# More visits to the wide chunks in the first stage of a transformer block kernel, and the key work moved behind it

## The chip, the cores and the metric

The kernel runs on one core of a Trainium2 chip. The metric is the device time of one execution in microseconds (us). The engines are called as the profile calls them: PE (TensorE, matrix products), DVE (VectorE), ACT (ScalarE), POOL (GpSimd) and SP (SyncE, whose queue issues nearly all DMAs here).

## What is computed

One layer of a diffusion backbone: 256 latent tokens `x` and 256 context tokens `ctx` of width 2048, all in fp32. The part that matters here, cut from the reference:

```python
shift, scale, gate = split(silu(c) @ w_mod + b_mod, 3)       # w_mod: 2048 x 6144
u   = layer_norm(x)   * (1 + scale)   + shift
u_c = layer_norm(ctx) * (1 + scale_c) + shift_c              # same w_mod, c_ctx
p   = u @ w_in                                               # all columns
p_c = u_c @ w_in[:, :N_KV]                                   # the key/value columns only
# columns: mLSTM q,k | mLSTM v | mLSTM gates | GQA k | GQA v | then o, z, q_b, z_b, g
q, k   = silu(conv3(qk_pre));  v = v_a                       # mLSTM inputs
k_b    = rope(rms_norm(k_b, k_norm_w))                       # GQA keys
h_a    = mlstm(q, k, v, gates);  o_attn = softmax(q_b k_b^T) v_b
out    = branch_merge(...) @ w_out;  x_new = layer_norm(ALPHA * x + gate * out)
```

The columns that both `x` and `ctx` need (mLSTM k, v and gates, GQA k and v) are the first stage of the kernel, up to about 419 us. The mLSTM q product, the heads, the attention, the merge and the output follow.

## The kernel before

A row tile is 128 of the 2048 rows that a product sums over; there are 16 of them (`KT`). An fp32 product is made of three products of rounded parts: weights and u are each split in a high half (`hi`, `whi`) and a low half (`lo`, `wlo`), and `three` (L336 to L338) or `three_b` (L341 to L343) multiplies high by high, high by low and low by high. A weight block holds two row tiles by 512 columns (128x1024, "wide"; 352 columns and 128x704 for w_kv, "narrow"), or one row tile where a visit begins or ends at an odd one. SP loads it (L312, tile `raw`, three buffers), ACT makes `whi` (L332), DVE makes `wlo` (L333); two blocks (`LEAD`) are split ahead of the one that PE multiplies.

The first stage has nine chunks of columns, in the list `chunks`: kv0, kv1, ka0, ka1, va0, va1, va2, va3, kv2. A product takes all 512 tokens, so a row tile of a chunk is 12 products (24 half as wide for ka). Each chunk sums in four PSUM banks (`four` takes the two sets of four in turn). Since u is made row tile by row tile, a chunk is visited twice: the first visits take row tiles 0 to `ENDS` (1, 1, 1, 3, 5, 6, 8, 9 and 10 of them), in which u is made; the second visits take the rest, in the same order of chunks. The first visit's sums are copied to SBUF by ACT, the second's are added there by DVE (`put`, L436 and L438). So the tenth visit, kv0's second, asks for row tiles 1 to 15 of u: all of them.

A row tile of u needs two columns of the modulation (shift and scale). For the first six (`MOD_PE`) PE makes them; for the ten others DVE does: four w_mod loads of 512 KB (`mod`, SP, L181), eight units (`mod_unit`, L221, tile `junk`), finishes (L227, L229), the normalised x (L254; for row tiles 12 to 15 it is loaded again as `xt`, L274), PE's transposes (`xT`, L286), and the split of u (ACT L298, DVE L299). These tasks are put in a list in program order: `end` is an estimate of PE's time by row tiles, and six tasks are given out for each `DT` us of it (11.5). `weave` spreads a visit's tasks over its products, four ticks a row tile. A scheduler then sets the order on each engine.

The 16 gate columns of the modulation are made in the same way, with two loads and two units each (`gate_task`), two columns in each second visit but the first (`GATES`). From the eleventh visit (`LATE`) on their loads take buffers from a later pool of three (`late`), in place of five. Three more pieces of work are woven into the second visits: `gates()` (mLSTM gate arithmetic, 13 steps), `conv_k` (one for each of eight heads, L637 to L641) and `keys()` (norm, rope and transposes of the GQA keys, ten steps, L657 to L705). The mLSTM q products (`w_qa`, two chunks of 16 row tiles, latent tokens only) come next with nothing woven in.

Of the kernel before, what the change touches and what calls it, by code (L numbers as in the profile page):

```python
# [17 lines left out]
KT = D // P  # L18
# [9 lines left out]
ALPHA = 2.0 ** 0.25  # L28
NEG = -1.0e30
BIG = 2064  # L30
ENDS = (1, 1, 1, 3, 5, 6, 8, 9, 10)
LATE = 1
GATES = (0, 2, 2, 2, 2, 2, 2, 2, 2)
MOD_PE = 6
AHEAD = 5
DEPTH = 3
# [1 line left out]
GAP = 1  # L38
LEAD = 2
SLOTS = (1, 2, 2, 4, 5)  # L40
T0, DT = 8.0, 11.5
SMALL = {1: 8, 2: 4, 4: 6, 16: 3}

C_ID, C_ONE, C_SEL, C_CAP, C_TRI = 0, P, 2 * P, 2 * P + 8, 5 * P + 8
# [4 lines left out]
def block_kernel(ctx: ExitStack, tc: tile.TileContext, a: dict, out: bass.AP):  # L49
# [33 lines left out]
    def acc(n):  # L83
        return ps.tile([P, 512], F32, tag="acc", name=nm(n))
# [4 lines left out]
    flip = [1]  # L89
# [216 lines left out]
    plan, early, ready = [], [], []  # L306
# [92 lines left out]
    def gemm_feat(w, kts, regions):  # L399


        for ks, _, _ in row_blocks(w, 512, kts):
            wh, wl = load_w()
            for b, k in enumerate(ks):
                for f in range(4):
                    tick()
                    need(k)
                    c0 = b * 512 + f * P
                    for s, o, first, last in regions[f]:
                        us = u[s][k // 4][:, k % 4]  # L410
                        three_b(o, wh[:, c0:c0 + P], wl[:, c0:c0 + P], turns(us[:, 0, :]),
                                turns(us[:, 1, :]), first and k == kts[0], last and k == kts[-1])
# [49 lines left out]
    def chunk_kv(c, kts, first):  # L462
# [5 lines left out]
        for t in range(4):  # L468
# [6 lines left out]
            else:  # L475
                put(vb[0][:, t, 160:512], tl[t][:, 0:352], first)

    chunks = [(chunk_kv, "w_kv", 0), (chunk_kv, "w_kv", 1), (chunk_ka, "w_ka", 0),
              (chunk_ka, "w_ka", 1), (chunk_va, "w_va", 0), (chunk_va, "w_va", 1),
              (chunk_va, "w_va", 2), (chunk_va, "w_va", 3), (chunk_kv, "w_kv", 2)]  # L480


    def row_tiles(g, c):
        return range(ENDS[c], KT) if g else range(ENDS[c])

    def prep_tasks(kt):

        ts = col_tasks(kt) if kt < MOD_PE else unit_tasks((kt, 16 + kt), (0, 1))
# [3 lines left out]
    def gate_task(j):  # L492
        return unit_tasks((j,), (0,)) + [lambda: mod_finish(j, (0,))]

    ln_stats()
    norm_x(0, 1)
    for g in range(2):
        for c, (_, w, i) in enumerate(chunks):
            plan.extend(b[1:] for b in row_blocks(a[w][i], 352 if w == "w_kv" else 512, row_tiles(g, c)))
    for ws in ([("w_qa", c)] for c in range(2)), ([("w_o", c), ("w_z", c)] for c in range(4)), \  # L500
            ([("w_qb", c), ("w_zb", c)] for c in range(4)), \
            ([("w_g", c), ("w_ba", c), ("w_g", 4 + c), ("w_bb", c)] for c in range(4)), \
# [1 line left out]
        for w, c in (x for l in ws for x in l):  # L504
            plan.extend(b[1:] for b in row_blocks(a[w][c], 512, range(KT)))
    tasks = queue(prep_tasks(0))
    between = [[] for _ in range(18)]
    for kt in range(1, MOD_PE):
        between[SLOTS[kt - 1]] += prep_tasks(kt)
    units = [t for kt in range(MOD_PE, KT) for t in prep_tasks(kt)]  # L510
    end, j = 0.0, 0
    for i in range(18):
        end += len(row_tiles(i // 9, i % 9)) * (1.8 if chunks[i % 9][1] == "w_kv" else 2.65)
        j0, j = j, max(j, min(len(units), math.ceil((end - T0) * 6 / DT)))
        between[i] = queue(mix(between[i], units[j0:j]))
    assert j == len(units)
# [398 lines left out]
    n = HEAD_STEPS  # L915
# [295 lines left out]
```

## Time and profile before

| | us |
|---|---|
| median of three runs | 1357.17 |
| lowest and highest | 1352.03, 1358.71 |
| profiled execution | 1356.43 |
| its span | 1354.7 |
| PE busy in the span | 1303.6 (96%) |
| DVE busy | 949.0 (70%) |
| ACT busy | 650.4 (48%) |

The profile is of one execution. The span runs from the first to the last instruction of the trace, and the 1.7 us between span and time lie around it. PE's busy time is a sum over listed instructions; matmuls overlap in the pipeline, so a busy PE isn't PE at its peak, and the granted clock (PEclk, 1.00 is the full one) has to be read beside it.

### The profile page before, as it was taken

What the parts mean: (1) busy time and instruction counts of PE and PEld (TensorE: products, weight loads), DVE (VectorE), ACT (ScalarE), POOL (GpSimd) and SP (SyncE); (2) the same over time, 40 slices, a digit from 0 to 9 for tenths busy, and PEclk for the clock granted to TensorE, in tenths of its full rate; (3) what the DMA queues carried; (4) which work ended last, traced back from release to release, by engine and by line L of the source; (5) the groups of instructions that cost most, each with busy time, mean ns of one, the idle gap of its engine ahead of it and who ended that gap; (6) DMA issues with size and microseconds to landing.
All of it is one profiled execution on the core that took longest, in us unless ns stands there. A gap on an engine that the chain in (4) does not pass through costs nothing. (4 is left out here: it accounts for less than half of the span.)

```text
span 1354.7 us, 19750 instructions
## 1 busy us (share of the span) xinstructions
PE 1303.6 (96%) x7613; PEld 1160.6 (86%) x7613; DVE 949.0 (70%) x1537; ACT 650.4 (48%) x929; POOL 44.9 (3%) x74
## 2 busy tenths in 40 slices
PE   5899999999999999999999999999999999999996
PEld 3678889999889988888889999898888888888885
DVE  6589997488745767788778778787555455544657
ACT  3544332154223667766665565666444444444441
POOL 0000000000100000100010000000000000000000
PEclk9999999999999999999999999999999999999998
DMA  8997768535435654445545354434756666576663
GB/s 301 331 326 246 234 210 290 201 124 196 161 110 162 190 193 157 164 167 169 190 148 186 128 169 143 153 125 160 215 200 202 201 195 208 191 281 219 213 219 121
DMA packets 77693, 264.16 MB, mean 195 GB/s; under 512 B 8904, under 2 KB 11608, under 8 KB 76960
## 3 DMA queue, kind: packets, MB, share of 16 engines
q1 hardware_dynamic: 75696, 256.19, 56.3%
q0 software_dynamic: 1296, 6.49, 1.4%
q8 instruction: 59, 0.97, 0.3%
q10 hardware_dynamic: 608, 0.24, 0.1%
q14 instruction: 34, 0.28, 0.1%
HBM read 260.75 MB, written 2.14 MB: 194 GB/s over the span
## 5 line engine op out<-in xcount | busy, mean ns | idle before, releaser
L333 DVE TENSOR_TENSOR wlo<-raw,whi 128x1024 fp32r<-128x1024 f32 (+2 forms) x374 | 444.7, 1192 | 296.0 <-ACT whi L332 295.7
L332 ACT CAST whi<-raw 128x1024 fp32r<-128x1024 f32 (+2 forms) x374 | 379.9, 1019 | 473.9 <-PE p L338 114.9
L336 PE MATMUL p<-whi,u 128*128 128x512 f32 (+1 forms) x448 | 158.7, 361 | 3.7 <-ACT u L298 2.8
L337 PE MATMUL p<-wlo,u 128*128 128x512 f32 (+1 forms) x448 | 159.5, 357 | 2.3 <-DVE wlo L333 2.1
L338 PE MATMUL p<-whi,u 128*128 128x512 f32 (+1 forms) x448 | 157.6, 355 | 0.0
L221 DVE SCALAR_TENSOR_TENSOR junk<-mod,sc 128x1024 bf16<-128x1024 f32 x112 | 134.2, 1219 | 10.0 <-DMA mod<-in_w_mod 9.7
L336 PEld LDWEIGHTS p<-whi,u 128*128 128x128 f32 x448 | 85.2, 192 | 15.5 <-ACT u L298 3.5
L337 PEld LDWEIGHTS p<-wlo,u 128*128 128x128 f32 x448 | 86.0, 192 | 11.2 <-DVE wlo L333 4.1
L338 PEld LDWEIGHTS p<-whi,u 128*128 128x128 f32 x448 | 85.9, 192 | 7.0 <-issue 0.4
L343 PE MATMUL p<-u,wlo 128*128 128x256 f32 x256 | 71.2, 278 | 2.3 <-DVE wlo L333 2.3
L341 PE MATMUL zb<-u,whi 128*128 128x256 f32 x256 | 72.1, 281 | 0.0
L341 PE MATMUL p<-u,whi 128*128 128x256 f32 x256 | 71.1, 278 | 0.0
L342 PE MATMUL p<-u,whi 128*128 128x256 f32 x256 | 70.8, 277 | 0.0
L343 PE MATMUL zb<-u,wlo 128*128 128x256 f32 x256 | 70.4, 275 | 0.0
L342 PE MATMUL zb<-u,whi 128*128 128x256 f32 x256 | 70.4, 275 | 0.0
L337 PE MATMUL z<-wlo,u 128*128 128x512 f32 x128 | 49.2, 384 | 4.3 <-DVE wlo L333 4.3
L337 PE MATMUL o<-wlo,u 128*128 128x512 f32 x128 | 49.1, 383 | 3.5 <-DVE wlo L333 3.4
L343 PEld LDWEIGHTS p<-u,wlo 128*128 128x128 f32 x256 | 49.5, 194 | 3.3 <-DVE wlo L333 2.5
L341 PEld LDWEIGHTS p<-u,whi 128*128 128x128 f32 x256 | 49.4, 193 | 0.4 <-issue 0.4
L336 PE MATMUL q<-whi,u 128*128 128x512 f32 x128 | 49.7, 388 | 0.0
L342 PEld LDWEIGHTS p<-u,whi 128*128 128x128 f32 x256 | 49.5, 193 | 0.0
L336 PE MATMUL ga<-whi,u 128*128 128x512 f32 x128 | 49.4, 386 | 0.0
(330 smaller groups left out, 3145.4 us busy)
## 6 DMA issues: line engine op xcount, KB each, us to landing
mod<-in_w_mod SPq DMA_DIRECT2D x96, 512.0 KB, 5.0
raw<-in_w_g SPq DMA_DIRECT2D x64, 512.0 KB, 4.3
raw<-in_w_o SPq DMA_DIRECT2D x32, 512.0 KB, 4.1
raw<-in_w_z SPq DMA_DIRECT2D x32, 512.0 KB, 4.2
raw<-in_w_qb SPq DMA_DIRECT2D x32, 512.0 KB, 3.9
raw<-in_w_zb SPq DMA_DIRECT2D x32, 512.0 KB, 3.5
raw<-in_w_ba SPq DMA_DIRECT2D x32, 512.0 KB, 3.5
raw<-in_w_bb SPq DMA_DIRECT2D x32, 512.0 KB, 4.1
```

Source lines behind the costliest of these rows:

```text
L221: nc.vector.scalar_tensor_tensor(junk, blk, 1.0, sc[v][:, hf * 1024:(hf + 1) * 1024], op0=ALU.mult, op1=ALU.mult, accum_out=mp[:, v, hf, j ...
L332: nc.scalar.copy(hi, src)
L333: nc.vector.tensor_tensor(lo, src, hi.bitcast(F32), op=ALU.subtract)
L336: mm(o, lhsT=xh, rhs=wh, start=start, stop=False)
L337: mm(o, lhsT=xh, rhs=wl, start=False, stop=False)
L338: mm(o, lhsT=xl, rhs=wh, start=False, stop=stop)
L341: mm(o, lhsT=wh, rhs=xh, start=start, stop=False)
L342: mm(o, lhsT=wh, rhs=xl, start=False, stop=False)
L343: mm(o, lhsT=wl, rhs=xh, start=False, stop=stop)
```

## The change

A table of 21 visits, (chunk, first row tile, end), takes the place of `ENDS`. The first nine are those of before. Then three wide chunks are visited again: va0 for row tiles 5 to 11, va1 for 6 to 12, va2 for 8 to 13. Only then comes kv0 for 1 to 15, then kv1, ka0 and ka1 as before, then third visits of va0 (12 to 15), va1 (13 to 15) and va2 (14 and 15), and va3 and kv2 as before. `DT` is 16 in place of 11.5. The later pool opens at the same place (kv1's second visit, now number 13). The gate columns are given out 3, 4, 3, 1, 1, 0, 2, 2 over the visits from kv1's on. The gate arithmetic is spread over kv1 to va0, `conv_k` of four heads goes to va3, of two to kv2, and the last two with all ten steps of `keys()` to the two q chunks, where the transposes now take PSUM banks of the other set (`flip[0] = 1`).

```diff
-ENDS = (1, 1, 1, 3, 5, 6, 8, 9, 10)
-LATE = 1
-GATES = (0, 2, 2, 2, 2, 2, 2, 2, 2)
+VISITS = ((0, 0, 1), (1, 0, 1), (2, 0, 1), (3, 0, 3), (4, 0, 5), (5, 0, 6), (6, 0, 8), (7, 0, 9),
+          (8, 0, 10), (4, 5, 12), (5, 6, 13), (6, 8, 14), (0, 1, 16), (1, 1, 16), (2, 1, 16),
+          (3, 3, 16), (4, 12, 16), (5, 13, 16), (6, 14, 16), (7, 9, 16), (8, 10, 16))
+LATE = 13
+GATES = (0,) * 13 + (3, 4, 3, 1, 1, 0, 2, 2)
...
-T0, DT = 8.0, 11.5
+T0, DT = 8.0, 16.0
...
-    for i in range(18):
-        end += len(row_tiles(i // 9, i % 9)) * (1.8 if chunks[i % 9][1] == "w_kv" else 2.65)
+    for i, (c, k0, k1) in enumerate(VISITS):
+        end += (k1 - k0) * (1.8 if chunks[c][1] == "w_kv" else 2.65)
...
-    for c, ts in enumerate(([], gs[:3], gs[3:6], [], gs[6:12], gs[12:] + cks[:4], cks[4:], ks[:3], ks[3:])):
-        between[9 + c] = mix(between[9 + c], ts)
+    for i, ts in enumerate((gs[:3], gs[3:6], gs[6:9], gs[9:11], gs[11:], [], cks[:4], cks[4:6])):
+        between[LATE + i] = mix(between[LATE + i], ts)
...
-        weave(between[i], 4 * len(kts))
-        fn(n, kts, i < 9)
+        weave(between[i], 4 * (k1 - k0))
+        fn(n, range(k0, k1), k0 == 0)
...
+    flip[0] = 1
+    for c, ts in enumerate((cks[6:] + ks[:4], ks[4:])):
         tl = [acc("qa") for _ in range(2)]
+        weave(ts, 32)
         gemm_feat(a["w_qa"][c], range(KT), regions_lat(tl))
+        flush()
```

The scheduler's order shows what moves. Up to about 64 us and from the second q chunk's middle on, the orders of the two kernels are the same on every engine. Names in the rows: `junk` is a unit, `mod` its loaded columns, `mv` a finish, `wlo` a split, `raw` a loaded block, `xt` an x tile; the numbers behind a name tell tiles apart and differ between the kernels.

**First place**, DVE, the normalisation of row tile 12's x. Before, it stands at the border of the first visits of va3 (the 128x512 block is its last) and kv2:

```order
L221 SCALAR_TENSOR_TENSOR junk_244_1291,mp_84<-mod_227_1187,sc_8_108 128x1024
L221 SCALAR_TENSOR_TENSOR junk_246_1305,mp_84<-mod_229_1201,sc_8_108 128x1024
L333 TENSOR_TENSOR wlo_248_1319<-raw_233_1226,whi_249_1320 128x512
L221 SCALAR_TENSOR_TENSOR junk_251_1325,mp_84<-mod_231_1215,sc_7_107 128x1024
L227 TENSOR_TENSOR mv_85<-mp_84 128x2
L221 SCALAR_TENSOR_TENSOR junk_251_1325,mp_84<-mod_231_1215,sc_8_108 128x1024
L221 SCALAR_TENSOR_TENSOR junk_254_1354,mp_84<-mod_236_1244,sc_7_107 128x1024
L333 TENSOR_TENSOR wlo_256_1365<-raw_240_1277,whi_257_1366 128x704
L254 TENSOR_SCALAR xt_252_1337<-xt_252_1337,ag0_148,rs0_147 128x128 x4
L221 SCALAR_TENSOR_TENSOR junk_254_1354,mp_84<-mod_236_1244,sc_8_108 128x1024
```

After, with kv2's first visit done, at the beginning of va0's second:

```order
L225 SCALAR_TENSOR_TENSOR junk_269_1497,mp_84<-mod_239_1307,sc_8_108 128x1024
L337 TENSOR_TENSOR wlo_266_1485<-raw_255_1402,whi_267_1486 128x512
L225 SCALAR_TENSOR_TENSOR junk_278_1534,mp_84<-mod_248_1338,sc_8_108 128x1024
L225 SCALAR_TENSOR_TENSOR junk_283_1557,mp_84<-mod_250_1364,sc_7_107 128x1024
L231 TENSOR_TENSOR mv_85<-mp_84 128x2
L225 SCALAR_TENSOR_TENSOR junk_283_1557,mp_84<-mod_250_1364,sc_8_108 128x1024
L337 TENSOR_TENSOR wlo_275_1528<-raw_260_1437,whi_276_1529 128x1024
L225 SCALAR_TENSOR_TENSOR junk_289_1598,mp_84<-mod_258_1420,sc_7_107 128x1024
L337 TENSOR_TENSOR wlo_280_1551<-raw_265_1483,whi_281_1552 128x1024
L258 TENSOR_SCALAR xt_284_1572<-xt_284_1572,ag0_148,rs0_147 128x128 x4
L225 SCALAR_TENSOR_TENSOR junk_289_1598,mp_84<-mod_258_1420,sc_8_108 128x1024
```

The normalisation now has two wide splits and a half one ahead of it among the units, where it had a half one and a narrow one.

**Second place**, DVE, the border of kv1 and ka0. The 128x512 block is ka0's first, the 128x704 block ahead of it kv1's last. Before:

```order
L221 SCALAR_TENSOR_TENSOR junk_426_2692,mp_84<-mod_424_2688,sc_7_107 128x1024
L333 TENSOR_TENSOR wlo_371_2134<-raw_361_2066,whi_372_2135 128x704
L221 SCALAR_TENSOR_TENSOR junk_431_2756,mp_84<-mod_425_2690,sc_7_107 128x1024
L227 TENSOR_TENSOR mv_85<-mp_84 128x1
L229 TENSOR_TENSOR mv_85<-mv_85,bm_74 128x1
L221 SCALAR_TENSOR_TENSOR junk_439_2876,mp_84<-mod_430_2754,sc_7_107 128x1024
L333 TENSOR_TENSOR wlo_374_2167<-raw_366_2100,whi_375_2168 128x512
L221 SCALAR_TENSOR_TENSOR junk_443_2938,mp_84<-mod_438_2874,sc_7_107 128x1024
L333 TENSOR_TENSOR wlo_381_2211<-raw_370_2132,whi_382_2212 128x1024
```

After:

```order
L225 SCALAR_TENSOR_TENSOR junk_446_2695,mp_84<-mod_438_2591,sc_7_107 128x1024
L337 TENSOR_TENSOR wlo_419_2472<-raw_408_2400,whi_420_2473 128x704
L225 SCALAR_TENSOR_TENSOR junk_451_2729,mp_84<-mod_445_2693,sc_7_107 128x1024
L231 TENSOR_TENSOR mv_85<-mp_84 128x1
L233 TENSOR_TENSOR mv_85<-mv_85,bm_74 128x1
L337 TENSOR_TENSOR wlo_423_2507<-raw_413_2436,whi_424_2508 128x512
L225 SCALAR_TENSOR_TENSOR junk_457_2818,mp_84<-mod_450_2727,sc_7_107 128x1024
L225 SCALAR_TENSOR_TENSOR junk_462_2852,mp_84<-mod_456_2816,sc_7_107 128x1024
L337 TENSOR_TENSOR wlo_430_2551<-raw_418_2470,whi_431_2552 128x1024
```

Two units and not one stand between the 128x512 split and the one behind it.

**Third place**, DVE, inside ka0's second visit. Before:

```order
L333 TENSOR_TENSOR wlo_392_2319<-raw_380_2209,whi_393_2320 128x1024
L227 TENSOR_TENSOR mv_85<-mp_84 128x1
L221 SCALAR_TENSOR_TENSOR junk_472_3196,mp_84<-mod_463_3123,sc_7_107 128x1024
L229 TENSOR_TENSOR mv_85<-mv_85,bm_74 128x1
L221 SCALAR_TENSOR_TENSOR junk_476_3229,mp_84<-mod_471_3194,sc_7_107 128x1024
L583 TENSOR_REDUCE m0_2575<-gc_389_2269 8x2
L227 TENSOR_TENSOR mv_85<-mp_84 128x1
L584 TENSOR_SCALAR m0_2575<-m0_2575 8x2
L229 TENSOR_TENSOR mv_85<-mv_85,bm_74 128x1
L221 SCALAR_TENSOR_TENSOR junk_489_3295,mp_84<-mod_487_3291,sc_7_107 128x1024
L221 SCALAR_TENSOR_TENSOR junk_495_3344,mp_84<-mod_488_3293,sc_7_107 128x1024
L333 TENSOR_TENSOR wlo_397_2377<-raw_386_2245,whi_398_2378 128x1024
```

After:

```order
L337 TENSOR_TENSOR wlo_448_2723<-raw_435_2585,whi_449_2724 128x1024
L231 TENSOR_TENSOR mv_85<-mp_84 128x1
L225 SCALAR_TENSOR_TENSOR junk_503_3314,mp_84<-mod_497_3246,sc_7_107 128x1024
L233 TENSOR_TENSOR mv_85<-mv_85,bm_74 128x1
L225 SCALAR_TENSOR_TENSOR junk_510_3386,mp_84<-mod_502_3312,sc_7_107 128x1024
L231 TENSOR_TENSOR mv_85<-mp_84 128x1
L225 SCALAR_TENSOR_TENSOR junk_520_3456,mp_84<-mod_518_3452,sc_7_107 128x1024
L233 TENSOR_TENSOR mv_85<-mv_85,bm_74 128x1
L337 TENSOR_TENSOR wlo_453_2783<-raw_442_2661,whi_454_2784 128x1024
L225 SCALAR_TENSOR_TENSOR junk_521_3483,mp_84<-mod_519_3454,sc_7_107 128x1024
```

Before, four units stand ahead of wlo_397 and none between it and the next splits; after, three stand ahead of wlo_453, as four do ahead of wlo_448 and three ahead of wlo_459.

## Rows read from the trace of the kernel before

**Rows 1.** The page, part 1: engine, busy us (share of the span), instructions.
```profile
PE 1303.6 (96%) x7613; PEld 1160.6 (86%) x7613; DVE 949.0 (70%) x1537; ACT 650.4 (48%) x929; POOL 44.9 (3%) x74
```

**Rows 2.** Windows: length, busy us (instructions) by engine, PEclk, DMA share, GB/s.
```profile
100.00:205.00 105.00, 99.14 (x553) 90.28 (x552) 99.16 (x204) 39.62 (x71) 0.62 (x1) 0.98 0.70 231
205.00:230.00 25.00, 25.00 (x173) 25.00 (x172) 19.87 (x51) 6.88 (x10) 0.00 (x0) 1.00 0.85 284
230.00:239.00 9.00, 6.74 (x45) 5.60 (x44) 7.64 (x17) 2.10 (x2) 0.00 (x0) 0.81 0.82 309
```

**Rows 3.** PE waits, 60 to 460 us: line, waited for, us, times, longest.
```profile
PE xT L286 <- DVE xt L254: 3.4, 3, 2.7
PE p L343 <- DVE wlo L333: 2.3, 1, 2.3
PE p L337 <- DVE wlo L333: 2.1, 3, 1.6
```

**Rows 4.** The windows again, two stretches at the lower clock.
```profile
149.40:152.90 3.50, 3.50 (x15) 3.50 (x14) 3.46 (x9) 1.19 (x3) 0.00 (x0) 0.51 0.61 208
234.70:238.30 3.60, 3.60 (x20) 2.78 (x19) 3.60 (x13) 0.32 (x1) 0.00 (x0) 0.53 0.89 311
```

**Rows 5.** PE timeline: start, us, line, op, names, form, [idle before, releaser].
```profile
144.54 0.38 PE L336 MATMUL p<-whi,u 128*128 128x512 f32 x1
...
145.62 0.38 PE L338 MATMUL p<-whi,u 128*128 128x512 f32 x1
148.66 0.30 PE L286 MATMUL xT<-cst,xt 128*128 128x128 f32 x1 [2.66 <-DVE xt L254]
...
172.24 0.31 PE L338 MATMUL p<-whi,u 128*128 128x352 f32 x1
172.39 0.31 PE L337 MATMUL p<-wlo,u 128*128 128x352 f32 x1
...
233.78 0.38 PE L343 MATMUL p<-u,wlo 128*128 128x256 f32 x1 [2.27 <-DVE wlo L333]
```

**Rows 6.** Timeline of DVE in kv2's first visit.
```profile
168.45 0.76 DVE L299 TENSOR_TENSOR u<-uf,u 128x256 fp32r<-128x256 f32 x2
169.13 1.22 DVE L221 SCALAR_TENSOR_TENSOR junk<-mod,sc 128x1024 bf16<-128x1024 f32 x1
...
170.27 1.22 DVE L221 SCALAR_TENSOR_TENSOR junk<-mod,sc 128x1024 bf16<-128x1024 f32 x1
```

**Rows 7.** Timeline of DVE around the border of kv1 and ka0.
```profile
222.81 0.89 DVE L333 TENSOR_TENSOR wlo<-raw,whi 128x704 fp32r<-128x704 f32 x1
...
231.36 1.23 DVE L221 SCALAR_TENSOR_TENSOR junk<-mod,sc 128x1024 bf16<-128x1024 f32 x1 [3.12 <-DMA mod<-in_w_mod]
...
232.51 1.22 DVE L333 TENSOR_TENSOR wlo<-raw,whi 128x1024 fp32r<-128x1024 f32 x1
...
247.57 1.23 DVE L221 SCALAR_TENSOR_TENSOR junk<-mod,sc 128x1024 bf16<-128x1024 f32 x1 [1.50 <-DMA mod<-in_w_mod]
```

**Rows 8.** DVE groups, 60:480: form, count | busy, mean ns | idle.
```profile
L333 DVE TENSOR_TENSOR wlo<-raw,whi 128x704 fp32r<-128x704 f32 x22 | 19.4, 885 | 9.7 <-ACT whi L332 9.7
L438 DVE TENSOR_TENSOR va<-p,va 128x512 f32<-128x512 f32 x16 | 10.3, 686 | 1.9 <-PE p L338 1.9
...
L639 DVE SCALAR_TENSOR_TENSOR cva<-kT,cv,cva 128x512 f32<-128x512 f32 x8 | 6.0, 749 | 0.1
...
L705 DVE COPY KT<-kT 128x512 f32<-128x512 f32 x4 | 4.3, 1068 | 0.5 <-PE kT L703 0.5
...
L667 DVE TENSOR_TENSOR rt<-kb,rope 128x512 f32<-128x512 f32 x2 | 1.6, 808 | 5.5 <-POOL rope L654 5.5
```

**Rows 9.** Timelines of SP and DVE: an x tile loaded and normalised.
```profile
142.53 0.39 SPq L274 DMA_DIRECT2D xt<-in_xc  x1
...
148.21 1.12 DVE L254 TENSOR_SCALAR xt<-xt,ag,rs 128x128 f32<-128x128 f32 x4 [1.16 <-DMA xt<-in_xc]
```

**Rows 10.** DMA issues, 200:260: form, count, KB each, median us to landing.
```profile
mod<-in_w_mod SPq DMA_DIRECT2D x17, 512.0 KB, 5.3
```

More of the change, by code (lines that the diff above doesn't have):

```diff
@@ L480, in block_kernel @@
               (chunk_va, "w_va", 2), (chunk_va, "w_va", 3), (chunk_kv, "w_kv", 2)]
-    def row_tiles(g, c):
-        return range(ENDS[c], KT) if g else range(ENDS[c])
     def prep_tasks(kt):
@@ L496, in block_kernel @@
     norm_x(0, 1)
-    for g in range(2):
-        for c, (_, w, i) in enumerate(chunks):
-            plan.extend(b[1:] for b in row_blocks(a[w][i], 352 if w == "w_kv" else 512, row_tiles(g, c)))
+    for c, k0, k1 in VISITS:
+        _, w, i = chunks[c]
+        plan.extend(b[1:] for b in row_blocks(a[w][i], 352 if w == "w_kv" else 512, range(k0, k1)))
     for ws in ([("w_qa", c)] for c in range(2)), ([("w_o", c), ("w_z", c)] for c in range(4)), \
@@ L506, in block_kernel @@
     tasks = queue(prep_tasks(0))
-    between = [[] for _ in range(18)]
+    between = [[] for _ in VISITS]
     for kt in range(1, MOD_PE):
@@ L714, in block_kernel @@
     cks = [lambda h=h: conv_k(h) for h in range(8)]
-    for c, ts in enumerate(([], gs[:3], gs[3:6], [], gs[6:12], gs[12:] + cks[:4], cks[4:], ks[:3], ks[3:])):
-        between[9 + c] = mix(between[9 + c], ts)
+    for i, ts in enumerate((gs[:3], gs[3:6], gs[6:9], gs[9:11], gs[11:], [], cks[:4], cks[4:6])):
+        between[LATE + i] = mix(between[LATE + i], ts)
     j = 32
-    for i in range(18):
-        c = i % 9
-        if i == 9 + LATE:
+    for i, (c, k0, k1) in enumerate(VISITS):
+        if i == LATE:
             mod_pool.__exit__(None, None, None)
             late.append(ctx.enter_context(tc.tile_pool(name="late", bufs=3)))
-        if i >= 9:
-            between[i] = mix(between[i], queue([t for k in range(GATES[c]) for t in gate_task(j + k)]))
-            j += GATES[c]
+        between[i] = mix(between[i], queue([t for k in range(GATES[i]) for t in gate_task(j + k)]))
+        j += GATES[i]
         fn, _, n = chunks[c]
-        kts = row_tiles(i // 9, c)
-        weave(between[i], 4 * len(kts))
-        fn(n, kts, i < 9)
+        weave(between[i], 4 * (k1 - k0))
+        fn(n, range(k0, k1), k0 == 0)
         flush()
@@ L734, in block_kernel @@
     nc.gpsimd.memset(qT[:, :, 257:258], 0.0)
-    for c in range(2):
+    flip[0] = 1
+    for c, ts in enumerate((cks[6:] + ks[:4], ks[4:])):
         tl = [acc("qa") for _ in range(2)]
+        weave(ts, 32)
         gemm_feat(a["w_qa"][c], range(KT), regions_lat(tl))
+        flush()
         for i in range(2):
```

## Prediction

> **What bounds the kernel now.** I read the page first. TensorE (PE) is busy for 96% of the span, DVE for 70% [rows 1]. So three things move the time: PE's work, PE's pauses, and stretches in which PE's clock falls. The change keeps every product: a chunk's row tiles are divided over more visits, and each is multiplied once. What can be won is the time that PE loses, and the next views say where that is.
>
> The table by windows sizes it [rows 2]. From 100 to 205 us PE is busy for 99.14 of 105.00 us and stands for 5.86; from 205 to 230 it doesn't stand; from 230 to 239 it stands for 2.26. The waits of PE agree: 3.4 us in three waits for the normalised x (xT), 2.1 us in three and 2.3 us in one for the low half of a weight block (wlo) [rows 3]. Two stretches of 3.5 and 3.6 us have a granted clock of 0.51 and 0.53, the lower of the two levels (1.2 of 2.4 GHz) [rows 4]. Each began about 1 us after a pause of over 2 us (2.66 us up to 148.66, 2.27 up to 233.78) [rows 5]. Such a stretch costs about half its length: 3.5 x 0.49 = 1.7 us and 3.6 x 0.47 = 1.7.
>
> A pause costs a little more than its listed idle time, because listed durations of matmuls overlap: a 128x352 product is listed at 0.31 us, but the next starts 0.15 later [rows 5], so the listed end ahead of a pause is some 0.16 too late. Six waits up to 205 us make 1.0 us.
>
> So the places are **100 to 205 us**, 5.9 + 1.7 + 1.0 = 8.6 us, and the **border of kv1 and ka0**, 230 to 239 us, 2.3 + 1.7 + 0.2 = 4.2 us. Together 12.8. The profiled execution took 1356.43 us, 0.7 under the median of the three runs (1357.17); I sum against it and take the result for the median.
>
> **Why PE stands from 100 to 205 us.** DVE is busy for 99.16 of these 105.00 us [rows 2]. A row tile of u that DVE modulates costs eight units at 1.14 us from start to start (169.13 to 170.27), a normalisation of 1.1 (listed, four instructions; for most row tiles it was done in bulk earlier, so I count 0.6), and 0.68 for its low halves (168.45 to 169.13), with some tenths for the finishes: about 11 us [rows 6, 9]. A block of two wide row tiles, listed at 1.22, costs it 1.14 us by starts, as a unit of the same size does; one of w_kv, listed at 0.885, some 0.81 [rows 6 to 8]. From the fifth visit (va0) to the end of kv0's second one DVE makes ten row tiles, 110 us, and splits 14 wide and 12.5 narrow blocks' worth, 16 + 10 us: 136 us. PE has 28 wide row tiles of 12 products at 0.216 us (six of them from 144.54 to 145.62) = 2.59 each, and 25 narrow ones at 12 x 0.15 = 1.8 [rows 5], with an estimated 10 us of transposes and modulation: 73 + 45 + 10 = 128 us. DVE is short of 8 us, and PE loses 8.6.
>
> **The change, part by part.**
>
> (1) *Three visits ahead of kv0's second.* They put 7 + 7 + 6 = 20 wide row tiles, 52 us of PE, before the place that needs all of u. DVE gets 10 wide splits with them (11.5 us) and 12 additions that the kernel before doesn't have; the same form is listed at 0.686 us [rows 8], so at most 12 x 0.69 = 8.2. The stretch becomes PE 180, DVE 136 + 11.5 + 8.2 = 156 us: DVE goes from 106% of PE's work to 87%, and PE sets the pace. The additions lie on DVE alone, and the next visit writes the other four banks, so PE waits for them only if DVE is a whole visit late. With the 24 us of slack they cost nothing; without it 8.2.
>
> (2) *DT 16 for 11.5.* DVE's queue now holds 11 us of work for u in each 16 us, and splits and additions between. This bears on the longest pause. At 148.66 PE waited for an x tile that DVE normalised at 148.21, after 1.16 us of waiting for its load, which SP had issued at 142.53, 5.7 us before [rows 5, 9]. A chain on the late side: DVE's units free the buffer, SP issues, the load lands, DVE normalises, PE transposes. In the changed order three to five units and two wide splits stand between (first fence on the order; PE needs the second of them, wlo_280, ahead of these transposes), 5.7 to 8 us at 1.14 each, about what the load took. I take all 8.6 us as gone and leave 0.5 for such a chain; bounds 0 and 2.
>
> (3) *The border of kv1 and ka0.* PE needed a block of w_ka from 231.5 and got it at 233.78 [rows 5]. One gate unit stood in front of the split on DVE (junk_443 before wlo_381, second fence), and it waited 3.12 us for its load [rows 7]. After the change two units stand there (junk_457, junk_462 before wlo_430). For it speaks that DVE arrives without the debt of u, so the last block of kv1, split at 222.81 [rows 7], some 6 us ahead of its end, should be split up to a block earlier, and the loads queued behind it on SP leave earlier too. Against it speaks the place right behind: the order has 13 units between the second and the seventh full block of ka0 where it had 5 (third fence shows the densest part), and SP's queue 14 w_mod loads among ka0's eight loads, 11 before. Seven units from 231.36 to 247.57, each behind its load, went at 2.7 us apiece [rows 7]; 12 of them ahead of wlo_459 need 32 us, and PE gets there after 29. With loads that land as from 200 to 260 us, 5.3 us each [rows 10], this place loses some 3 us of PE; if the three buffers overlap fully, none; with a pause of over 2 us and a half-clock stretch, 6. I take 2.5 for border and burst together, against the 4.2 of before: 1.7 gained; bounds -2 and +4.2.
>
> (4) *Key work beside the q products.* It leaves the short visits for a stretch where DVE has no u to make. There it is much: four copies of 1.07 us, six conv steps of at most 0.75 and 18 smaller products of at most 0.81 [rows 8] make 23 us at the most, and 16 splits 18.4 us. PE has 384 products of 128x256 there, half of a 512's 0.216 us each [rows 5], 41.5 us, and 16 transposes. DVE is at most as full as PE, with two blocks of lead, so the price is what the queue's order does. Bounds 0 and two splits that are late, 2.4 us; I take 1. The transposes use the banks that the q sums leave free.
>
> (5) *One weight block in halves* (a visit begins at an odd row tile): a DMA and a split more, no byte more. With the 24 us of slack, nothing; uncovered, half a split, 0.6.
>
> **Sum.** 8.6 - 0.5 + 1.7 - 1 = 8.8; counted by starts and not by listed idle times, the two places hold some 1 to 2 us more, so I take 10: 1356.4 - 10 = 1346.4. The case's own range: 8.6 - 2 - 2 - 2.4 = 2.2 is its worst sum, too unlikely all at once; two of the three give 5, 1351; all 12.8 and 2 of counting error give 1341.5.
>
> **Rivals.**
>
> *Same: the gate burst takes the gain back.* If ka0's blocks each wait for the unit chain (6 lost) and the q products for rope and conv (2.4), 8.6 - 2 + 4.2 - 6 - 2.4 is 2.4: 1354. Against it: from 205 to 230 us, with units among narrow blocks, PE doesn't stand at all [rows 2].
>
> *Same: PE's work is the time.* PE is 96% busy [rows 1] and its work is unchanged, so by the busy share alone the time stays at 1356. Against it: 7.8 us of waits and 7 us at half clock are hidden in that share [rows 3, 4], and DVE is as full as PE where the waits lie [rows 2]. The Trainium skill, Perfetto Trace Analysis, "Identifying the Most-Contended Engine", says to optimise the engine of highest occupancy first; by that rule the change, which takes nothing from PE, would give 1356. The windows of 100 to 205 us disagree with it here.
>
> *Slower: ka0 is bound by its loads.* The split at 222.81 and the one at 232.51 lay 9.7 us apart [rows 7], for blocks of 5.2 us of PE (24 x 0.216). If the chain (a unit's buffer, SP's queue, the load) sets each of six blocks of ka0 at 9.7, they lose 6 x 4.5 = 27 us: 1356.4 - 8.1 + 27 - 4.2 = 1371. It decides when SP's order makes each block's own load wait behind two or more w_mod loads, and these for units that wait in turn. Against it: seven units took 2.7 us each, so 13 make 35 us for six blocks, not 58.
>
> *The change doesn't do what it says.* The scheduler could gather units ahead of splits; the order shows splits spread among units in the three new visits, so this has no share of its own.
>
> **How the numbers follow.** Forecast 0.64, burst 0.17, PE's work 0.06, slower 0.08, more than 15 gained 0.05. A measurement of this kernel can tell about 0.5%, 6.8 us, from no change, so faster means under 1350. Nearly all of the forecast's range and the larger gain lie there, 0.67; the two rivals without gain and the forecast's edge make 0.25; 0.08 is slower. The range of 1340 to 1354 reaches into the burst and leaves out the slower case and the rest of the others.
>
> **What would show it.** From 100 to 205 us PE at full with clock 1.00, no wait for xT, and DVE waiting for whi there in place of PE for wlo. The border keeps a pause of 1 to 3 us, or ka0 shows one at its sixth full block. I am wrong if ka0 shows repeated waits for wlo, if the q products pause, or if PE still stands in va0 to kv2 or in the three new visits.

## The result

The changed kernel took 1347.89 us (median of 6 runs, 1343.92 to 1350.41) against 1357.53 us for the kernel before (6 runs in all, 1352.03 to 1361.24): a ratio of 0.9931, 95% interval 0.9911 to 0.995. In a later comparison of the two it was 1350.83 against 1356.33 us, 0.9961 (0.9947 to 0.9976). The prediction was 1346.4 us, 1340 to 1354.

The page of after, part 1, as [rows 1]: PE has 6.1 us less busy time over a span that is 7.0 us shorter, DVE 6.8 us more.

```profile
PE 1297.5 (96%) x7613; PEld 1157.8 (86%) x7613; DVE 955.8 (71%) x1550; ACT 651.4 (48%) x930; POOL 45.8 (3%) x74
```

The windows of after: from 100 us to the end of the stretch in which u is made (now 225 us), then up to the end of the first stage and the q products. The columns are those of [rows 2].

```profile
100.00:160.00 60.00, 60.00 (x319) 54.51 (x318) 49.63 (x94) 24.83 (x42) 0.00 (x0) 1.00 0.64 218
160.00:225.00 65.00, 62.56 (x312) 55.01 (x311) 63.07 (x124) 19.13 (x30) 0.19 (x1) 1.00 0.59 195
225.00:360.00 135.00, 135.00 (x1069) 132.67 (x1068) 101.55 (x205) 45.30 (x59) 6.08 (x11) 1.00 0.67 230
360.00:451.00 91.00, 91.00 (x646) 86.38 (x645) 69.88 (x101) 40.56 (x50) 4.17 (x4) 1.00 0.47 154
```

PE stands for 2.4 us in the 125 us to 225, where it stood for 5.9 in 105 us [rows 2], and not at all after. PEclk is 1.00 throughout: neither half-clock stretch [rows 4] stands in this profile. DVE is at 83% in the first of these windows (49.63 of 60 us), with slack, and at 97% in the second. The waits of PE from 60 to 470 us, as [rows 3]:

```profile
PE p L341 <- DVE wlo L337: 2.4, 3, 1.7
PE p L340 <- ACT whi L336: 0.7, 1, 0.7
```

No wait for xT is left, and none at the border (p L347, which was p L343). The longest of the three that remain is at kv0's second visit; here is PE's row, and DVE's rows ahead of it:

```profile
221.23 0.42 PE L341 MATMUL p<-wlo,u 128*128 128x352 f32 x1 [1.68 <-DVE wlo L337]
...
217.90 2.48 DVE L442 TENSOR_TENSOR va<-p,va 128x512 f32<-128x512 f32 x4
220.30 0.88 DVE L337 TENSOR_TENSOR wlo<-raw,whi 128x704 fp32r<-128x704 f32 x1
```

The four additions of va2's added visit (217.90) stand right in front of the split (220.30) for which PE waits until 221.23. At the border of kv1 and ka0, DVE still waits for a load, 1.97 us, but the split behind it is done at 275.7 us, just when PE comes to it:

```profile
273.38 1.23 DVE L225 SCALAR_TENSOR_TENSOR junk<-mod,sc 128x1024 bf16<-128x1024 f32 x1 [1.97 <-DMA mod<-in_w_mod]
...
274.53 1.22 DVE L337 TENSOR_TENSOR wlo<-raw,whi 128x1024 fp32r<-128x1024 f32 x1
```

Single profiles differ outside the part that the change moves. To compare that part, I take the **stage time**: from the start of PE's 301st instruction (60.1 us before; up to there all kernels here have one order) to the start of the first product `o` behind the q products. Between the two every kernel has the same number of PE instructions. Before it is 402.2 us, after 390.6: **11.6 us less**. In the second profile of the changed kernel it is 391.7, 10.5 us less. The profiled execution of after (1350.41 us, the slowest of its first six) gives 3.8 us of that back from the q products to PE's last product, where both kernels have the same order; waits for a block of w_g at 1211 us, 1.0 and 0.8 us, and a half-clock stretch of 3.4 us right behind them, that the profile of before doesn't have, are part of it.

### The profile page after: what moved, and what is told of

Its sections match the earlier page's. It is cut to its first block, busy times and chain, and to the rows that moved or that the text cites. A ratio compares the mean times of both kernels' runs of the same rounds, so it can differ in the third digit from the quotient of the medians.

```text
span 1347.7 us, 19754 instructions
## 1 busy us (share of the span) xinstructions
PE 1297.5 (96%) x7613; PEld 1157.8 (86%) x7613; DVE 955.8 (71%) x1550; ACT 651.4 (48%) x930; POOL 45.8 (3%) x74
## 5 line engine op out<-in xcount | busy, mean ns | idle before, releaser
L337 DVE TENSOR_TENSOR wlo<-raw,whi 128x1024 fp32r<-128x1024 f32 (+3 forms) x375 | 444.9, 1189 | 290.8 <-ACT whi L336 290.3
L336 ACT CAST whi<-raw 128x1024 fp32r<-128x1024 f32 (+3 forms) x375 | 380.1, 1017 | 469.5 <-PE p L342 127.6
L341 PE MATMUL p<-wlo,u 128*128 128x512 f32 (+1 forms) x448 | 158.3, 353 | 2.4 <-DVE wlo L337 2.4
L341 PEld LDWEIGHTS p<-wlo,u 128*128 128x128 f32 x448 | 85.3, 190 | 10.3 <-DVE wlo L337 3.5
L347 PE MATMUL p<-u,wlo 128*128 128x256 f32 x256 | 70.6, 276 | 0.0
L347 PE MATMUL zb<-u,wlo 128*128 128x256 f32 x256 | 70.4, 275 | 0.0
L341 PE MATMUL o<-wlo,u 128*128 128x512 f32 x128 | 48.9, 382 | 3.8 <-DVE wlo L337 3.8
L341 PE MATMUL z<-wlo,u 128*128 128x512 f32 x128 | 49.0, 383 | 3.1 <-DVE wlo L337 3.1
L340 PE MATMUL gb<-whi,u 128*128 128x512 f32 x128 | 49.3, 385 | 1.0 <-ACT whi L336 1.0
L341 PE MATMUL gb<-wlo,u 128*128 128x512 f32 x128 | 49.2, 384 | 0.8 <-DVE wlo L337 0.8
L347 PEld LDWEIGHTS p<-u,wlo 128*128 128x128 f32 x256 | 49.1, 192 | 0.8 <-issue 0.8
L340 PE MATMUL o<-whi,u 128*128 128x512 f32 x128 | 49.2, 384 | 0.7 <-ACT whi L336 0.7
```

The source lines that it names most:

```text
L336: nc.scalar.copy(hi, src)
L337: nc.vector.tensor_tensor(lo, src, hi.bitcast(F32), op=ALU.subtract)
L340: mm(o, lhsT=xh, rhs=wh, start=start, stop=False)
L341: mm(o, lhsT=xh, rhs=wl, start=False, stop=False)
L347: mm(o, lhsT=wl, rhs=xh, start=False, stop=stop)
```

## The experiments

The theory: while u is made, DVE has more to do than PE, so PE waits; the added visits and the slower pace (DT) give it time. Below, "wait" is listed idle time of PE with its releaser, 60 to 470 us. Stage times come from single profiles, medians from all runs of a kernel; one group of kernels ran on one chip.

| kernel | median us (runs) | kernel before there | ratio, 95% | stage time us, and against before |
|---|---|---|---|---|
| changed | 1347.89 (6) | 1357.53 | 0.9931, 0.9911 to 0.995 | 390.6, -11.6 |
| e1_two_visits | 1354.67 (10) | 1354.18 | 0.9999, 0.9983 to 1.0015 | 398.4, -3.8 |
| e2_visits_only | 1350.43 (10) | 1354.18 | 0.9973, 0.9952 to 0.9993 | 393.3, -8.9 |
| e3_before_half_units | 1351.21 (10) | 1354.18 | 0.9976, 0.9956 to 0.9995 | 392.8, -9.4 |
| e4_after_half_units | 1341.76 (4) | 1354.18 | 0.9915, 0.9883 to 0.9946 | 387.8, -14.4 |
| e5_dt115 | 1354.64 (10) | 1354.51 | 1.0003, 0.9987 to 1.0018 | 397.6, -4.6 |
| e6_one_extra | 1359.2 (6) | 1354.51 | 1.004, 1.002 to 1.006 | 402.4, +0.2 |
| e7_four_extra | 1352.5 (10) | 1354.51 | 0.9992, 0.9972 to 1.0012 | 398.0, -4.2 |
| e8_dt145 | 1350.82 (10) | 1354.51 | 0.9971, 0.9951 to 0.9991 | 392.7, -9.5 |
| f1_after_again | 1350.83 (9) | 1356.33 | 0.9961, 0.9947 to 0.9976 | 391.7, -10.5 |
| f2_no_adds | 1344.34 (6) | 1356.33 | 0.9911, 0.989 to 0.9932 | 388.9, -13.2 |
| f3_four_extra_banks | 1354.17 (12) | 1356.33 | 0.9982, 0.9965 to 0.9998 | 394.0, -8.1 |
| f4_ka1_first | 1356.05 (12) | 1356.33 | 1.0003, 0.9987 to 1.0019 | 397.7, -4.5 |

The differences of medians are 1.2 to 6.4 us less good than those of stage times, mostly 4 to 6. A large part of that is the clock.

The profile of before has its two half-clock stretches inside the stage, 2 x 1.7 = 3.4 us lost; e6 loses as much there, e7 and f4 1.7, the others nothing. But several of these (e1, e2, e3, e5, e7, f1, f3) have a half-clock stretch ahead of the stage instead, at 50 to 58 us, in work that all kernels share; it brings the 301st instruction to 62.8 to 64.4 us in place of 60. And the mean granted clock, which is on record for each run, doesn't rise with the change: 0.9938 over f1's nine runs, 0.9940 over the 26 of before beside them, where 3.4 us would be 0.0025. So the half clock's share of a stage difference, 3.4 us for the changed kernel, is no gain that the change is shown to give; without it f1's stage is 7.1 us better, for 5.5 in the medians. What is left of the offset stays open.

**e1_two_visits.** The two visits of before with the new gate and key work.

```diff
-          (8, 0, 10), (4, 5, 12), (5, 6, 13), (6, 8, 14), (0, 1, 16), (1, 1, 16), (2, 1, 16),
-          (3, 3, 16), (4, 12, 16), (5, 13, 16), (6, 14, 16), (7, 9, 16), (8, 10, 16))
-LATE = 13
-GATES = (0,) * 13 + (3, 4, 3, 1, 1, 0, 2, 2)
+          (8, 0, 10), (0, 1, 16), (1, 1, 16), (2, 1, 16),
+          (3, 3, 16), (4, 5, 16), (5, 6, 16), (6, 8, 16), (7, 9, 16), (8, 10, 16))
+LATE = 10
+GATES = (0,) * 10 + (3, 4, 3, 1, 1, 0, 2, 2)
...
-T0, DT = 8.0, 16.0
+T0, DT = 8.0, 11.5
```

> The changed kernel without the three added visits: two visits to each chunk and DT 11.5 as before, but the gate columns, the gate arithmetic and the key work placed as after the change. Theory 1 (DVE short of time while u is made; the added visits give PE other work): PE stands from 100 to 205 us as before, 5 to 7 us of listed idle time with a half-clock stretch, the border at 230 to 239 us can go either way by 4 us; 1352 to 1358 us. Rival 1 (the gain comes from the moved gate and key work): 1346 to 1350 us, with nothing lost at the border.

Its waits of PE:

```profile
PE xT L290 <- DVE xt L258: 5.5, 3, 3.2
PE p L341 <- DVE wlo L337: 2.3, 4, 1.6
```

As theory 1 has it: the waits for xT are longer than before (5.5 us for 3.4), and the median is that of before. But the wait at the border is gone here too, without the added visits. So the new gate placement alone is enough to cure the border, and it isn't where the rest comes from. The stage's 3.8 us are hardly a gain: these two lines make 7.8 us of waits, as much as the three of [rows 3], and 3.4 of the 3.8 us are the half clock, which this profile doesn't have in the stage, though its longest pause is longer than that of before. Here are the end of that pause and the clock behind it:

```profile
152.35 0.30 PE L290 MATMUL xT<-cst,xt 128*128 128x128 f32 x1 [3.25 <-DVE xt L258]
...
152.30:156.00 3.70, 3.65 (x26) 3.68 (x26) 3.67 (x10) 0.60 (x2) 0.00 (x0) 1.00 0.50 175
```

**e2_visits_only.** The other half: the visits and DT, gates and key work as before.

```diff
-GATES = (0,) * 13 + (3, 4, 3, 1, 1, 0, 2, 2)
+GATES = (0,) * 13 + (2, 2, 2, 2, 2, 2, 2, 2)
...
-    for i, ts in enumerate((gs[:3], gs[3:6], gs[6:9], gs[9:11], gs[11:], [], cks[:4], cks[4:6])):
+    for i, ts in enumerate((gs[:3], gs[3:6], [], gs[6:12], gs[12:] + cks[:4], cks[4:], ks[:3], ks[3:])):
...
-    flip[0] = 1
-    for c, ts in enumerate((cks[6:] + ks[:4], ks[4:])):
+    for c in range(2):
...
-        weave(ts, 32)
...
-        flush()
```

> The added visits and DT 16, but gate columns two in each visit from kv1 on and the key work in the first stage as before. Theory 1: within 3 us of the changed kernel, 1345 to 1351 us, PE idle under 3 us from 100 to 240 us. Rival 1: 1354 to 1358 us.

```profile
PE p L341 <- DVE wlo L337: 2.5, 3, 1.7
PE kT L703 <- DVE ky L698: 1.0, 2, 0.7
PE kT L703 <- DVE ky L677: 0.9, 1, 0.9
```

The waits of the stretch up to 225 us are those of after, 2.5 us, and the border has none: the visits alone do most of it, and either part cures the border. New are three waits for the key transposes, 1.9 us: in the visits of va3 and kv2 DVE has gate units and additions between the key steps, and PE comes to the transposes first. Moving the key work to the q products buys these waits, 1.6 to 2.7 us of stage time (393.3 against 391.7 and 390.6). The times don't tell the two apart: 0.9973 here and 0.9961 in f1, with intervals that overlap.

**e3_before_half_units and e4_after_half_units.** Half of each unit that makes u is left out, in the kernel before and in the changed one (half of the modulation sums is missing from the result).

```diff
+        w = 512 if len(vs) == 2 else 1024
         for v in vs:
             nc.vector.scalar_tensor_tensor(
-                junk, blk, 1.0, sc[v][:, hf * 1024:(hf + 1) * 1024],
+                junk[:, :w], blk[:, :w], 1.0, sc[v][:, hf * 1024:hf * 1024 + w],
```

> The kernel before, with each of the 80 units that make u covering 512 of its 1024 columns (half of the modulation sum is left out; loads are as before), some 0.55 us less each, 44 us less on DVE. Theory 1: the waits of PE from 100 to 205 us fall from 5.5 us to under 1.5 and the half-clock stretch there goes, 1345 to 1350 us. Rival 2 (the x loads and SP's queue make PE wait, not DVE's work): waits for xT stay at 2 to 3.4 us, 1353 to 1357 us.

> The changed kernel with the same half units. Theory 1: DVE has slack already, so only the rest goes (2.4 us of waits from 160 to 225 us): 1344 to 1348 us, within 4 us of the kernel before with half units. Rival 3 (the added visits help by something other than DVE's time): as far below the kernel before with half units as the change itself, 8 to 11 us.

The waits of e3, then the one of e4:

```profile
PE p L338 <- DVE wlo L334: 2.3, 2, 2.1
...
PE p L344 <- DVE wlo L334: 0.6, 1, 0.6
PE p L337 <- ACT u L299: 0.6, 1, 0.6
```

```profile
PE p L341 <- ACT whi L337: 0.7, 1, 0.7
```

With loads as before and only DVE's work less, no wait for xT is left, and the stage is 9.4 us shorter, of which 3.4 us are the half clock. So PE waited for DVE's time, not for SP's queue (rival 2). Shorter units free the load buffers sooner as well; this run doesn't tell that part apart. 3.5 us of waits stay, more than expected, and 1351.21 us is a little above the range expected. e4 leaves only the wait that all kernels have at 75 us. Its stage is 5.0 us shorter than e3's (387.8 and 392.8), of which 3.5 are the waits that e3 keeps. The 9.4 us between the medians are what rival 3 named; in the two profiles 4.2 us more lie at the start (the 301st instruction at 64.4 and 60.2 us) and 4.9 from the q products to PE's last product. So theory 1 holds in the stage, 1 us outside its bound; for the medians rival 3 can't be excluded.

**e5_dt115.** The change with DT 11.5 (`T0, DT = 8.0, 11.5`), nothing else.

> The changed kernel with DT back at 11.5: the units are handed out as fast as before, beside wide row tiles. Theory 1 with an in-order queue: 11 us of work for u and some 2.5 us of splits and additions in each 11.5 us make DVE late while u is made, so PE waits from 100 to 190 us as before (6 to 12 us lost) and the added visits come too late to help: 1352 to 1359 us. Rival (the added visits alone are enough, since they put work ahead of the place that needs all of u): within 3 us of the changed kernel, 1345 to 1351 us.

```profile
PE xT L290 <- DVE xt L258: 4.2, 3, 2.6
PE p L341 <- DVE wlo L337: 2.3, 3, 1.5
```

As expected of an in-order queue: up to 205 us the waits are no shorter than before (6.5 us for 5.5), and only the border's is gone. Of the stage's 4.6 us 3.4 are, as in e1, the half clock that this profile doesn't have there. Units that are handed out faster than DVE can do them stand ahead of the splits whatever is waiting further on. Up to 225 us the added visits give nothing without the slower pace.

**e6_one_extra.** Only va0's added visit, DT 12.5.

```diff
-          (8, 0, 10), (4, 5, 12), (5, 6, 13), (6, 8, 14), (0, 1, 16), (1, 1, 16), (2, 1, 16),
-          (3, 3, 16), (4, 12, 16), (5, 13, 16), (6, 14, 16), (7, 9, 16), (8, 10, 16))
-LATE = 13
-GATES = (0,) * 13 + (3, 4, 3, 1, 1, 0, 2, 2)
+          (8, 0, 10), (4, 5, 12), (0, 1, 16), (1, 1, 16), (2, 1, 16),
+          (3, 3, 16), (4, 12, 16), (5, 6, 16), (6, 8, 16), (7, 9, 16), (8, 10, 16))
+LATE = 11
+GATES = (0,) * 11 + (3, 4, 3, 1, 1, 0, 2, 2)
...
-T0, DT = 8.0, 16.0
+T0, DT = 8.0, 12.5
```

> Only va0's added visit (row tiles 5 to 11, 18 us of PE), DT 12.5 so that the units end at the same share of the way. By the sums of theory 1 DVE has 143 us of work beside 146 us of PE there, 98%: 2 to 5 us of the 8.6 stay lost, 1349 to 1353 us. If any surplus is enough: 1345 to 1349 us. If the gain needs all three: 1354 or more.

Here are its waits, and the two DVE rows ahead of the longest one, which ends at 194.4 us:

```profile
PE p L341 <- DVE wlo L337: 6.5, 3, 4.8
PE xT L290 <- DVE xt L258: 2.3, 3, 1.5
PE p L347 <- DVE wlo L337: 1.4, 1, 1.4
```

```profile
191.66 1.88 DVE L442 TENSOR_TENSOR va<-p,va 128x512 f32<-128x512 f32 x3
193.46 0.88 DVE L337 TENSOR_TENSOR wlo<-raw,whi 128x704 fp32r<-128x704 f32 x1
```

No gain, the third of the outcomes named: 4.7 us slower in the medians. The sums say 98%, and that is not enough. The end of the work for u and the additions of the added visit meet at kv0's border, where a half block of 12 products of 0.15 us covers 1.8 us; the split behind the additions is 4.8 us late, and a half-clock stretch of 6.8 us (3.4 lost) begins at 193.3 us. One added visit moves the wait there and doesn't take it away.

**e7_four_extra and f3_four_extra_banks.** A fourth added visit (va3, row tiles 9 to 14), DT 17.5; and the same with the PSUM banks of the q sums and the key transposes exchanged.

```diff
+          (8, 0, 10), (4, 5, 12), (5, 6, 13), (6, 8, 14), (7, 9, 15), (0, 1, 16), (1, 1, 16), (2, 1, 16),
+          (3, 3, 16), (4, 12, 16), (5, 13, 16), (6, 14, 16), (7, 15, 16), (8, 10, 16))
...
-    flip[0] = 1
+    flip[0] = 0
-        tl = [acc("qa") for _ in range(2)]
+        tl = [aux("qa") for _ in range(2)]
```

> A fourth added visit (va3, row tiles 9 to 14), DT 17.5. Theory 1: DVE at 83% of PE there; what is left of PE's waits from 160 to 225 us (2.4 us) goes or stays: 1345 to 1349 us, no more than 3 us below the changed kernel. If the gain grows with the added visits: 1343 or less.

> Four added visits as tried before, with the q sums in the banks of the other set and the key transposes in the first, since an even number of visits ends in the set that the q sums took. Theory 1b (the 3.3 us wait at the start of the q products is for kv2's additions in the same banks): this wait goes and with it some 4 to 5 us, 1346 to 1350 us, the waits of 2.2 us at ka0 stay. Otherwise: 1351 to 1355 us, and the q products wait as before.

The wait of e7 at the q products, and f3's waits there:

```profile
PE qa L345 <- DVE vb L442: 3.3, 1, 3.3
```

```profile
PE qa L347 <- DVE wlo L337: 1.4, 2, 0.8
...
PE qa L345 <- ACT whi L336: 0.8, 1, 0.8
```

With 22 visits the last one sums in the banks that the q sums take, and they wait for its additions; DVE had waited itself, for `kr` from POOL. Exchanging the banks takes that wait away, as theory 1b has it, and 4.0 us of stage time, 1.7 of them a half-clock stretch that e7 has at 415 us. But three waits for weight blocks, 2.2 us, come in the q products instead, and the median stays at 1354.17 us, in the second range: the 4 to 5 us that were expected didn't come. More visits than three bring nothing.

**e8_dt145.** `T0, DT = 8.0, 14.5`.

> The changed kernel with DT 14.5: the units end earlier, so that kv0's visit begins with a freer DVE. Theory 1: the pause of 1.7 us at 219 us goes, and small waits from 100 to 180 us come if DVE gets full there: 1345 to 1350 us, within 3 us of the changed kernel.

Waits of 2.6 us for wlo in four places (the longest 1.4) and a stage of 392.7 us: no better than DT 16, and 0.8 us above the range expected. The pause at 222 us didn't go (1.4 us).

**f1_after_again and f2_no_adds.** The changed kernel again, and without the 12 additions of the added visits (these parts of the sums are missing).

```diff
     def put(dst, src, first):
+        if drop[0]:
+            return
...
+        drop[0] = 9 <= i < 12
```

> The changed kernel once more, beside the three below on one chip. 0.990 to 0.996 of the kernel before; in the profile PE waits for wlo at kv0's second visit (near 221 us), 1.5 to 1.8 us, and nowhere between 225 and 360 us.

> The changed kernel without the 12 additions of the three added visits (these parts of the sums are left out). Theory 1a (the four additions that stand ahead of the second split of kv0's second visit cost PE 1.7 us there, the other eight lie in DVE's slack): the wait near 221 us falls under 0.5 us, the rest is as in the changed kernel, so the q products begin 1.5 to 3 us earlier. Rival (the prediction's step: all 12 are hidden, the units alone make that wait): the wait stays at 1.2 us or more.

f1's waits, then f2's:

```profile
PE p L341 <- DVE wlo L337: 2.5, 3, 1.7
PE p L347 <- DVE wlo L337: 0.8, 1, 0.8
```

```profile
PE p L347 <- DVE wlo L337: 0.6, 1, 0.6
PE p L341 <- DVE wlo L337: 0.4, 1, 0.4
```

The wait at kv0's border (1.7 us) goes with the additions, so they make it and not the units alone; the stage is 1.6 us shorter than after's and 2.7 shorter than f1's. The medians differ by 6.5 us (1344.34 and 1350.83), more than was expected; the mean clock of f2's six runs is higher (0.9948 for 0.9938, some 1.4 us), and the rest isn't explained. f1 also has a wait of 0.8 us in ka0, against what was expected: the border is at its edge. Its ratio of 0.9961 is just above the 0.990 to 0.996 expected.

**f4_ka1_first.** A try for a faster one.

```diff
-          (8, 0, 10), (4, 5, 12), (5, 6, 13), (6, 8, 14), (0, 1, 16), (1, 1, 16), (2, 1, 16),
-          (3, 3, 16), (4, 12, 16), (5, 13, 16), (6, 14, 16), (7, 9, 16), (8, 10, 16))
-LATE = 13
-GATES = (0,) * 13 + (3, 4, 3, 1, 1, 0, 2, 2)
+          (8, 0, 10), (4, 5, 12), (5, 6, 13), (6, 8, 14), (3, 3, 16), (0, 1, 16), (1, 1, 16), (2, 1, 16),
+          (4, 12, 16), (5, 13, 16), (6, 14, 16), (7, 9, 16), (8, 10, 16))
+LATE = 14
+GATES = (0,) * 14 + (3, 4, 2, 2, 1, 2, 2)
...
-T0, DT = 8.0, 16.0
+T0, DT = 8.0, 17.5
...
-    for i, ts in enumerate((gs[:3], gs[3:6], gs[6:9], gs[9:11], gs[11:], [], cks[:4], cks[4:6])):
+    for i, ts in enumerate((gs[:3], gs[3:6], gs[6:9], gs[9:11], gs[11:], cks[:4], cks[4:6])):
```

> A try for a faster one: ka1's second visit (31 wide row tiles' worth of split products, 13 row tiles) is moved ahead of kv0's, DT 17.5, the gate columns given to one visit less. If a wide block's cover takes the waits at kv0's border (2.9 us of PE from 160 to 225 us in the changed kernel): 1 to 3 us below the changed kernel. If the gate loads in a shorter row of visits are late: waits at ka0 of 2 us and more, the same as the changed kernel or up to 5 us slower.

```profile
PE kT L703 <- DVE ky L677: 4.3, 1, 4.3
PE p L347 <- DVE wlo L337: 2.6, 3, 1.4
...
PE p L341 <- DVE wlo L337: 0.2, 1, 0.2
```

Of the waits at blocks of w_va and w_kv (L341) 0.2 us is left, but those at blocks of w_ka (L347) make 2.6 us in three places, and the key transposes wait 4.3. Not faster. No kernel here that computes the whole result is shown to beat the changed one.

## Why the prediction was right

The time came out 1.5 us above the forecast, and the stage lost 11.6 and 10.5 us of its time where 10 was taken; in the second comparison the medians differ by 5.5 us. By its steps:

- **Where the time is lost, and why: right.** The waits for xT went when DVE had less to do (e3) and stayed when it had not (e1, e5).
- **The half clock, 1.7 us in each place: not shown as a gain.** I counted the stretch up to 205 us as won and the border's in the 4.2. After has neither, but e1 and e5 keep pauses of 3.25 and 2.63 us for xT and go on at full clock, and the mean clock of the runs is the same with the change and without. So the profile of before was one execution with such stretches in these places. What the waits give is surer: 8.5 us of listed waits in the stage before and 3.1 after, each with the 0.7 at 75 us that every kernel has.
- **Step (1), the additions "cost nothing": wrong.** They cost 1.7 us of waiting at kv0's second visit, where four of them stand ahead of a split and the cover is one narrow row tile. The slack of 24 us over the stretch was there (83% of DVE in the first half), but not at that place: DVE is at 97% from 160 to 225 us. Of the 8.6 us some 2.4 + 3 x 0.16 = 2.9 are left, and I had left 0.5. Two of the three waits are in the added visits, a sign that I had named for being wrong: 0.36 us at 166 and 0.40 at 201 us, small.
- **Step (2), the chain of the x load: right**, no wait for xT is left. That DT was needed with the visits I had costed as one piece; e5 shows that without it the waits up to 205 us stay.
- **Step (3), border and gate burst: mis-sized.** I kept 2.5 us of loss; it was 0 and, in f1, 0.8. At the border the split is ready in time although its unit waits 1.97 us for a load; that DVE came earlier there is argued, and e1, where the border is free without the added visits, speaks for the order of the gate work as well. The burst in ka0, priced at 3 us, cost nothing. Here are the first and the last of the 12 units ahead of the sixth full block, that block's split, and PE's first product with it:

```profile
278.93 1.22 DVE L225 SCALAR_TENSOR_TENSOR junk<-mod,sc 128x1024 bf16<-128x1024 f32 x1
...
301.32 1.22 DVE L225 SCALAR_TENSOR_TENSOR junk<-mod,sc 128x1024 bf16<-128x1024 f32 x1
...
303.45 1.20 DVE L337 TENSOR_TENSOR wlo<-raw,whi 128x1024 fp32r<-128x1024 f32 x1
...
307.86 0.28 PE L347 MATMUL p<-u,wlo 128*128 128x256 f32 x1
```

The units went at 22.4 / 11 = 2.0 us apiece where I took 2.7, and PE came to the block 4.4 us after the start of its split; from ka0's beginning it was 34.6 us, not 29, since I had left out PE's own gate sums (L559) in between. My 2.7 was misread: of the seven units from 231.36 to 247.57 only three waited for their loads, and three splits and eight additions for kv1 lie among them. SP's w_mod loads among ka0's eight are 15 in the trace of after and 13 in that of before, where I wrote 14 and 11.
- **Step (4), the key work: 1 us taken, none measured.** It is a gain, compared with leaving it where it was (e2: 1.9 us of waits).
- **The rivals.** PE's work as the time: refuted, with the same products both comparisons are faster, and the stage has 5.4 us less of listed waits. The gate burst and the slower case: not seen. The slower case was also priced too high: between the splits at 222.81 and 232.51 us stands that of ka0's half block, at 227.55, so the 9.7 us were for a block and a half.

So two terms were wrong in opposite directions, 2.4 us too good in (1) and 2.5 and 1 too bad in (3) and (4), and the sum was near: in that, and in what it took for the half clock, there is luck. Two of its smaller sums are slightly off and change nothing: 16 splits at 1.14 us are 18.2 us, not 18.4, and two of the three worst terms, with the third as taken, leave 3.6 to 5.9 us, where I wrote 5.

## What to carry to other kernels

An engine that is 96% busy can still have a stage that another engine limits: compare both engines' work stage by stage, and move work of the waiting engine into the stage where the other is short. In an in-order queue the room alone did nothing here up to 205 us; the pace at which the other work is handed out has to follow it (e5). Then look at each border between pieces for what stands directly in front of the next operand: slack over a stretch doesn't cover a short piece at its end (e6, and the 1.7 us here). And when two single profiles are compared, take the clock out first: 3.4 of the 11.6 us here were the clock, and the clock of all the runs doesn't bear them out.

## What the runs showed of the hardware

- **Pauses of PE and its clock.** At the start of the kernels PE waits for a load near 50 us. The profile of before has 1.47 us of idle time there and full clock afterwards. f1 has half clock behind its own (2.05 us), in the same work; the windows from 50 to 55 us, first before, then f1:

```profile
50.00:55.00 5.00, 4.51 (x46) 4.21 (x39) 3.23 (x8) 1.99 (x5) 0.15 (x2) 1.00 0.98 388
```

```profile
50.00:55.00 5.00, 4.53 (x24) 4.30 (x21) 3.21 (x8) 1.99 (x5) 0.00 (x0) 0.50 1.01 406
```

The 301st instruction starts 2.7 us later with it (62.8 for 60.1 us), in work that the change doesn't touch: a difference of the same size as several effects here. The profile of after has the lower clock (0.53) from 25 to 30 us instead and 1.00 here; why a run takes the one or the other isn't settled. Nor does the length of a pause settle it: after 2.66 us [rows 5] the clock of before fell to half, after 3.25 us that of e1 did not.

- **A POOL product that can be late while DVE works.** `kr`, one product on POOL of 128x16, took 2.94 us in the kernel before. In f4 it is listed at 6.44:

```profile
411.63 6.44 POOL L131 TENSOR_TENSOR kr<-rs,powc 128x16 f32<-128x16 f32 x1 [35.39 <-DVE rs L130]
```

```profile
413.38 1.28 DVE L337 TENSOR_TENSOR wlo<-raw,whi 128x1024 fp32r<-128x1024 f32 x1
414.51 0.75 DVE L676 TENSOR_TENSOR rt<-rt,ry 128x512 f32<-128x512 f32 x1
418.10 0.69 DVE L677 TENSOR_TENSOR ky<-rt,kr 128x512 f32<-128x512 f32 x1 [2.84 <-POOL kr L131]
```

DVE's products run back to back up to 415.3 us; then DVE waits for `kr`, and 2.84 us later it is there, and the same 2.84 us stand in e7 and f3. So `kr` seems to have taken its whole time after DVE had stopped. But in e2 DVE was busy through all of `kr`, and the product that needs it (L677) started without a wait:

```profile
387.00 3.85 POOL L131 TENSOR_TENSOR kr<-rs,powc 128x16 f32<-128x16 f32 x1 [45.21 <-DVE rs L130]
...
387.00:390.80 3.80, 3.80 (x19) 3.32 (x19) 3.80 (x8) 0.78 (x1) 3.79 (x1) 1.00 0.69 211
...
391.21 0.68 DVE L677 TENSOR_TENSOR ky<-rt,kr 128x512 f32<-128x512 f32 x1
```

The Trainium skill, SBUF — State Buffer, "SBUF: two separate sides", says that DVE and GpSimd share a pair of ports as an exclusive lock, held for a whole instruction, also where the DVE operation has two inputs in SBUF. The rows of f4 would fit that; those of e2 don't, since there products of both, DVE's with two operands in SBUF, ran side by side. What holds `kr` up in f4, e7 and f3 stays open.
